# A two-layer encoder on one core: the probabilities of layer 1's attention turned by DMA instead of by TensorE, with the memory heads' halves, two output blocks and the memory loads moved beside it

## The chip, the core and the metric

The kernel runs on one core of a Trainium2 chip. Its time is the device time of one execution in microseconds (us). An execution taken with the profiler is described by its span, from the first to the last instruction, and by its own time, which is a little longer. Matrix products run on TensorE (PE in the profile, its weight loads PEld), elementwise work on VectorE (DVE) and ScalarE (ACT), a little on GpSimd (POOL). Weights are loaded by DMAs that SyncE (SP) issues; DMA transposes are issued from ACT's queue; small tables and the memory tokens come through POOL's queue. Every engine works through its own list of instructions strictly in order: an instruction that waits holds up all that stand behind it on its engine.

## What is computed

A trunk of two layers over 256 tokens of width 2048, all in f32. Layer 0 mixes tokens by a gated spatial product, layer 1 by grouped-query attention: 12 query heads of 128, 4 key and value heads, per-head RMS norm and rotary tables. Each layer also attends with 4 heads over 256 memory tokens; token heads and memory heads share one input and one output projection, and a SwiGLU feed-forward part follows.

```
h = rms_norm(x, g_mix[l])
z = h @ w_in_b                       # layer 1: queries, keys, values, memory queries
tok_out = softmax(q @ k.T * scale) @ v            # 12 heads, 256 x 256 each
kv = rms_norm(mem, g_mem[l]) @ w_mem_kv[l]
mem_out = softmax(q_mem @ k_mem.T * scale) @ v_mem    # 4 heads
x = x + concatenate([tok_out, mem_out]) @ w_out[l]
x = x + (silu(gate) * up) @ w_down[l]             # gate, up = rms_norm(x, g_ffn[l]) @ w_gate_up[l]
```

## The kernel before, in words

**Products.** f32 products are made from three fp32r products of halves (`matmul3`, L183 to L188): the high half of a times the high half of b (L186), low times high (L187), high times low (L188). The high half is a cast copy on ACT, the low half the difference on DVE. For activations that is `split` (L180 on ACT, L181 on DVE).

**Weights.** A weight matrix comes in blocks of 512 columns. A block is loaded as four *units* of four 128-row pieces, 1 MB each; I write in_b 23 for the last unit of the sixth block of `w_in_b`. `halves` makes a unit's two halves in two steps of 128x1024: `whi` on ACT (L270), then `wlo` on DVE (L271). Both have three tiles, so the halves of a unit can only be written when TensorE is through with the unit three before it. A unit is 24 matmuls of 128x512 into the two accumulators of its `Linear`. There are four accumulator banks in all, two for each block, so a block can start only when the block before the last has been read out of its banks. Four further banks (`m` in the names) serve transposes, scores and weighted sums.

**Layer 1's input stage.** In order: keys (in_b 0 to 3), values (4 to 7), three groups of four token heads called c0, c1 and c2 here (8 to 19), memory queries (20 to 23), then the memory keys (mem_kv 8 to 11), the memory values (mem_kv 12 to 15), and the four blocks of `w_out` (out 16 to 31). For each group of heads `queries` reads the accumulators (squares on ACT, L466; rotary on DVE, L474, L479 and L481, which free the banks), and `attend` then runs four kinds of steps: queries turned, scores with softmax (row maximum L557 on DVE, a product on POOL L558, exponentials L562 on ACT, reciprocal L566 and scaling L568 on DVE), probabilities turned, and weighted sums (`weigh`). Two heads make a step. The probabilities of a token head are turned by four TensorE transposes of 128x128 (L585) into an `m` bank, and split from there. Those of the memory heads go by DMA: `turned` (L194) copies the f32 words apart into two planes of 16 bits (128x1024, L199), issues a DMA transpose from ACT (L200), and three steps later copies back (L205).

**The order.** `later(n, step)` puts a step n *ticks* behind, two ticks to a weight unit; this sets the order in which the program states its work and its priorities. A scheduler then lays out each engine's list by its own costs, and that list is fixed: on the chip nothing is overtaken.

**Tiles.** A room of 36 tiles of 128x512 (`a` in the names) holds the stage's values. A second pool of 16 tiles (`h`) holds the normed input; after the last input unit (in_b 23) has been multiplied these are free.

Of the kernel before, what the change touches and what calls it, by code (L numbers as in the profile page):

```python
# [11 lines left out]
F32R = mybir.dt.float32r  # L12
# [5 lines left out]
P = 128  # L18
# [37 lines left out]
def encoder(ctx: ExitStack, tc: tile.TileContext, x, x_t, mem, mem_t, columns, w_in_a, g_v_a, spatial_t, w_in_b,  # L56
# [18 lines left out]
    def big(dt=F32, shape=None):  # L75
        return room["p"].tile(shape or [P, NB], dt, tag="a", name=nm("a"))
# [13 lines left out]
    def misc():  # L90
        if room["banks"] == 2:
            return banks2()[:, 0]
        return room["m"].tile([P, NB], F32, tag="m", name=nm("m"))

    def v4(a):
        return a.rearrange("p (c n) -> p c n", n=P)
# [80 lines left out]
    def split(src, shape, home=None):  # L177

        hi, lo = [(home or big)(F32R, shape) for _ in range(2)]
        nc.scalar.copy(hi, src)  # L180
        nc.vector.tensor_tensor(lo, src, hi.bitcast(F32), ALU.subtract)  # L181
        return hi, lo

    def matmul3(out, a, b, start, stop):

        nc.tensor.matmul(out, lhsT=a[0], rhs=b[0], start=start, stop=False)  # L186
        nc.tensor.matmul(out, lhsT=a[1], rhs=b[0], start=False, stop=False)  # L187
        nc.tensor.matmul(out, lhsT=a[0], rhs=b[1], start=False, stop=stop)  # L188
# [118 lines left out]
    def linear(parts, w, n0, units=kd, nk=KD):  # L307
        return Linear(parts, w, n0, nk).run(units)
# [202 lines left out]
            res.append(qn)  # L511
        return res

    def heads_T(qn, dma=False):

        hi = [big(F32R, [P, 2, S]) for _ in range(2)]
        lo = [big(F32R, [P, 2, S]) for _ in range(2)]

        def halves_of(t, whole):
            ts = slice(t * P, (t + 1) * P)  # L520
            for pr in range(2):
                src = whole[:, 2 * pr:2 * pr + 2, :]
                nc.scalar.copy(hi[pr][:, :, ts], src)
                nc.vector.tensor_tensor(lo[pr][:, :, ts], src, hi[pr][:, :, ts].bitcast(F32), ALU.subtract)

        for t in range(NT):
            if dma:
                turned(qn[t], 3, lambda whole, t=t: halves_of(t, whole), True, nc.vector.tensor_copy)
            else:
                tp = misc()  # L530
                transpose4(qn[t], tp)
                halves_of(t, v4(tp))
        return hi, lo

    def attend(qn, waits, keys, values, kv_of, kc0, parts, dma=None, home=None):


        qn, rows = qn
        by_head = rows.rearrange("p (t h) -> p h t", t=NT)
        st = {}  # L540

        def head(p, h):
            return p[0][h // 2][:, h % 2, :], p[1][h // 2][:, h % 2, :]

        def queries_T():
            st["qT"] = heads_T(qn, dma and home is None)

        def scores(pr):
            for h in (2 * pr, 2 * pr + 1):
                kp_ = head(keys(), kv_of(h))  # L550
                qp_ = head(st["qT"], h)
                sc = misc()
                for t in range(NT):
                    ts = slice(t * P, (t + 1) * P)
                    matmul3(sc[:, t * S:(t + 1) * S], (qp_[0][:, ts], qp_[1][:, ts]), kp_, True, True)
                nmx = small(2)
                nc.vector.tensor_reduce(nmx, sc.rearrange("p (t k) -> p t k", t=NT), AX.X, ALU.max, negate=True)  # L557
                nc.gpsimd.tensor_tensor(nmx, nmx, by_head[:, h], ALU.mult)  # L558
                pe = big()
                sm = small(2)  # L560
                for t in range(NT):
                    nc.scalar.activation(pe[:, t * S:(t + 1) * S], sc[:, t * S:(t + 1) * S], AF.Exp,  # L562
                                         bias=nmx[:, t:t + 1], scale=rows[:, 4 * t + h:4 * t + h + 1],
                                         accum_out=sm[:, t:t + 1])
                rcp = small(2)
                nc.vector.reciprocal(rcp, sm)  # L566
                for t in range(NT):
                    nc.vector.tensor_scalar(pe[:, t * S:(t + 1) * S], pe[:, t * S:(t + 1) * S], rcp[:, t:t + 1], None,  # L568
                                            ALU.mult)
                st["p", h] = pe  # L570

        def turn(pr):
            for h in (2 * pr, 2 * pr + 1):
                pn = st["p", h]
                if dma:
                    def halves_of(whole, h=h):
                        hi, lo = split(whole.rearrange("p (t k) n -> p k t n", t=NT), [P, 2, NT, P], home)
                        st["t", h] = [a.rearrange("p k t n -> p (k t n)") for a in (hi, lo)]

                    turned(pn, 3, halves_of, True, nc.vector.tensor_copy, home)  # L580
                    continue
                pt = misc()
                for t in range(NT):
                    for kc in range(2):
                        nc.tensor.transpose(pt[:, kc * S + t * P:kc * S + (t + 1) * P],  # L585
                                            pn[:, t * S + kc * P:t * S + (kc + 1) * P], ident)
                st["t", h] = split(pt, [P, NB])

        def weigh(pr):
            V = values()  # L590
            po = misc()
            for hh in range(2):
                h = 2 * pr + hh
                kv = kv_of(h)
                phi, plo = st["t", h]
                for kc in range(2):
                    vhi, vlo = V[kc]
                    vs, ks = slice(kv * P, (kv + 1) * P), slice(kc * S, (kc + 1) * S)
                    matmul3(po[:, hh * S:(hh + 1) * S], (vhi[:, vs], vlo[:, vs]), (phi[:, ks], plo[:, ks]),
                            kc == 0, kc == 1)  # L600
            hi, lo = split(po.rearrange("p (h s) -> p h s", h=2), [P, 2, S])
            for hh in range(2):
                for t in range(NT):
                    ts = slice(t * P, (t + 1) * P)
                    parts.put(kc0 + 2 * pr + hh, t, hi[:, hh, ts], lo[:, hh, ts])

        later(waits[0], queries_T)
        for wait, f in zip(waits[1:], (scores, turn, weigh)):
            for pr in range(2):
                later(wait + pr, lambda f=f, pr=pr: f(pr))  # L610

    def scaled(acc, r):

        res = []
        for t in range(NT):
            hi = big(F32R)
            lo = big(F32R)
            nc.scalar.activation(hi, acc[t], AF.Copy, scale=r[t])
            nc.vector.scalar_tensor_tensor(lo, acc[t], r[t], hi.bitcast(F32), ALU.mult, ALU.subtract)
            res.append((hi, lo))  # L620
        return res
# [2 lines left out]

    class Memory:
        def __init__(self, l):
            self.l, self.parts, self.r = l, Parts(), mem_r
            if l == 0:
                self.norm = Norm()

# [23 lines left out]
        def keys(self):  # L654
            acc = linear(self.parts, w_mem_kv[self.l], 0)
            kn = head_norm(acc, self.r, ghead[f"mk{self.l}"])

            def turn():
                self.kT = heads_T(kn, not self.l)
            later(4, turn)  # L660

        def values(self):
            self.V = scaled(linear(self.parts, w_mem_kv[self.l], NB), self.r)

        def attend(self, acc, r, parts, waits, dma, home=None):
            attend(queries(acc, r, ghead[f"mq{self.l}"]), waits, lambda: self.kT, lambda: self.V, lambda h: h, TOK // P,
                   parts, dma, home)

    def add_residual(acc, j, norm, g, parts, dma, copy=nc.scalar.copy):

# [20 lines left out]
    for l in range(DEPTH):  # L691
# [121 lines left out]
                    later(1 + t, lambda u=u, t=t, c=c: turn_u(u, t, c))  # L813
        else:
            w = w_in_b[0]
            own = {}
            load_tables(1)
            m.prep(20, 2)
            acc = linear(hT, w, TOK)
            kn = head_norm(acc, norm.r, ghead["k"], True)  # L820

# [11 lines left out]
            own["v"] = scaled(linear(hT, w, TOK + MEMW), norm.r)  # L833
            for c in range(3):
                acc = linear(hT, w, c * NB)
                attend(queries(acc, norm.r), (5, 6, 11, 14), lambda: own["k"], lambda: own["v"],
                       lambda h, c=c: (4 * c + h) // 3, 4 * c, cat)
            m.attend(linear(hT, w, TOK + 2 * MEMW), norm.r, cat, (4, 13, 16, 20), True, kept)
            m.keys()
            m.values()  # L840

        hF = Parts()
        norm = Norm()
        units = kd if l else [(12, KC4), (0, KC4), (4, KC4), (8, KC4)]
        for j in range(4):
            acc = linear(cat, w_out[l], j * NB, units)
            add_residual(acc, j, norm, gslice("ffn", l), hF, j < 3, nc.scalar.copy if l else nc.vector.tensor_copy)
        room.clear()
        scope.close()
# [130 lines left out]
```

## Time and profile before

| | us |
|---|---|
| median of 3 runs | 1986.66 (1985.84 to 1986.9) |
| the profiled execution's own time | 1988.33 |
| its span | 1986.5 |
| PE busy | 1975.7 (99%) |
| DVE busy | 1645.0 (83%) |
| ACT busy | 1217.9 (61%) |
| POOL busy | 95.7 (5%) |

The granted TensorE clock was 1.000 over the span. In the rows of a profile, `x16 | 10.9, 680` after an instruction's shape means 16 instructions, 10.9 us of busy time and 680 ns mean duration of one; behind the second bar stands how long the engine idled just before them and what ended that. Durations of consecutive instructions overlap a little on the chip; where I lay instructions end to end I use the distance of their starts. Layer 1's input stage stands at about 989 to 1320 us of the span.

### The profile page before, as it was taken

To read this page: it belongs to the slowest core of one execution; us is meant where nothing else is said; L and a number is where in the kernel's file an instruction comes from. 1 tells how busy PE (TensorE), PEld (TensorE's weight loads), DVE (VectorE), ACT (ScalarE), POOL (GpSimd) and SP (SyncE) were. 2 spreads that over 40 slices of the span, in tenths; PEclk is the share of its full clock that TensorE was granted. 3 is DMA by queue.
4 is the path that set the end of the run, shared out by engine and by line. 5 is a ranking of instruction groups with operands and counts; after the bars stand their busy time and mean duration, and the time that the engine had idled before them with its cause. 6 is when DMAs were issued, how large, how long until landed. Compare 5 with 4: busy or idle time off the path is not lost.

```text
span 1986.5 us, 24053 instructions
## 1 busy us (share of the span) xinstructions
PE 1975.7 (99%) x8897; PEld 1636.8 (82%) x8897; DVE 1645.0 (83%) x1755; ACT 1217.9 (61%) x1461; POOL 95.7 (5%) x148
## 2 busy tenths in 40 slices
PE   9999999999999999999999999999999999999998
PEld 7888888888888888888888888888888888888887
DVE  6658778998889989898676866699989889898987
ACT  8756455766546665466766665756665466654673
POOL 2300001000000000000020110010000000000000
PEclk9999999999999999999999999999999999999999
DMA  9867865576775777767866545657767667686674
GB/s 349 300 191 203 242 212 190 189 217 216 231 244 186 220 217 239 235 191 232 239 201 197 168 140 175 217 191 220 226 198 246 212 208 233 195 251 215 202 219 140
DMA packets 287719, 426.99 MB, mean 215 GB/s; under 512 B 93904, under 2 KB 94160, under 8 KB 287600
## 3 DMA queue, kind: packets, MB, share of 16 engines
q1 hardware_dynamic: 199808, 387.62, 58.8%
q10 hardware_dynamic: 82800, 20.91, 6.3%
q0 software_dynamic: 4992, 16.91, 3.8%
q8 instruction: 70, 1.15, 0.2%
q14 instruction: 49, 0.40, 0.1%
HBM read 394.45 MB, written 2.10 MB: 200 GB/s over the span
## 4 chain that ended last, share of the span: by engine, by line
PE 94%; DMA 2%; DVE 2%; ACT 1%; issue 1%; SPq 0%; DVEq 0%; ACTq 0%
PE acc L188 27%; PE acc L186 26%; PE acc L187 26%; PE m L188 5%; PE m L186 5%; PE m L187 5%; DMA a<-a 1%; DVE wlo L271 1%; DMA raw<-in_w_in_a 1%; PE m L192 0%; ACT whi L270 0%; PE m L722 0%; ACT junk L212 0%; PE m L585 0%; DVE T L379 0%
## 5 line engine op out<-in xcount | busy, mean ns | idle before, releaser
L271 DVE TENSOR_TENSOR wlo<-raw,whi 128x2048 fp32r<-128x2048 f32 (+2 forms) x466 | 841.4, 1821 | 202.9 <-ACT whi L270 198.8
L270 ACT CAST whi<-raw 128x2048 fp32r<-128x2048 f32 (+2 forms) x466 | 705.9, 1535 | 434.3 <-PE acc L187 294.5
L186 PE MATMUL acc<-whi,h 128*128 128x512 f32 x1440 | 561.6, 390 | 1.7 <-ACT whi L270 1.7
L187 PE MATMUL acc<-whi,h 128*128 128x512 f32 x1440 | 560.7, 389 | 0.0
L188 PE MATMUL acc<-wlo,h 128*128 128x512 f32 x1440 | 514.8, 390 | 0.1
L186 PE MATMUL acc<-whi,a 128*128 128x512 f32 x999 | 388.3, 390 | 1.0 <-DVE x L457 1.0
L187 PE MATMUL acc<-whi,a 128*128 128x512 f32 x999 | 388.6, 389 | 0.0
L188 PE MATMUL acc<-wlo,a 128*128 128x512 f32 x999 | 365.6, 390 | 0.4 <-DVE wlo L271 0.3
L188 PEld LDWEIGHTS acc<-wlo,h 128*128 128x128 f32 x1440 | 270.3, 188 | 57.9 <-DVE wlo L271 2.0
L186 PEld LDWEIGHTS acc<-whi,h 128*128 128x128 f32 x1440 | 270.4, 188 | 57.4 <-ACT whi L270 2.3
L187 PEld LDWEIGHTS acc<-whi,h 128*128 128x128 f32 x1440 | 270.4, 188 | 55.4
L188 PEld LDWEIGHTS acc<-wlo,a 128*128 128x128 f32 x999 | 187.5, 188 | 40.7 <-DVE wlo L271 2.1
L186 PEld LDWEIGHTS acc<-whi,a 128*128 128x128 f32 x999 | 187.6, 188 | 39.8 <-issue 1.4
L187 PEld LDWEIGHTS acc<-whi,a 128*128 128x128 f32 x999 | 187.6, 188 | 38.8
L270 ACT CAST whi<-T 128x1536 fp32r<-128x1536 f32 x93 | 137.8, 1481 | 119.2 <-PE acc L187 98.7
L271 DVE TENSOR_TENSOR wlo<-T,whi 128x1536 fp32r<-128x1536 f32 x93 | 162.9, 1751 | 4.7 <-PE acc L188 4.7
L379 DVE TENSOR_TENSOR T<-raw 128x1024 f32<-128x1024 f32 x93 | 113.4, 1219 | 19.8 <-DMA raw<-in_w_gate_up 19.7
L186 PE MATMUL m<-whi,a 128*128 128x512 f32 x284 | 110.7, 390 | 0.0
L187 PE MATMUL m<-whi,a 128*128 128x512 f32 x284 | 110.5, 389 | 0.0
L188 PE MATMUL m<-wlo,a 128*128 128x512 f32 x284 | 110.5, 389 | 0.0
L457 DVE TENSOR_TENSOR e<-acc,e 128x512 f32<-128x512 f32 x120 | 79.0, 684 | 1.5 <-PE acc L188 1.3
L205 ACT COPY sg<-a 128x1024 uint16<-128x1024 uint16 x44 | 51.5, 1171 | 30.7 <-DMA a<-a 30.5
(162 smaller groups left out, 1528.0 us busy)
## 6 DMA issues: line engine op xcount, KB each, us to landing
raw<-in_w_gate_up SPq DMA_DIRECT2D x352, 512.0 KB, 4.4
raw<-in_w_down SPq DMA_DIRECT2D x176, 512.0 KB, 5.1
raw<-in_w_out SPq DMA_DIRECT2D x32, 1024.0 KB, 5.3
raw<-in_w_in_a SPq DMA_DIRECT2D x24, 1024.0 KB, 8.0
raw<-in_w_in_b SPq DMA_DIRECT2D x24, 1024.0 KB, 5.1
raw<-in_w_mem_kv SPq DMA_DIRECT2D x16, 1024.0 KB, 5.2
x<-e POOLq DMA_DIRECT2D x16, 512.0 KB, 5.0
a<-in_mem_t POOLq DMA_DIRECT2D x16, 256.0 KB, 5.9
```

Of the source, the lines that this page charges most:

```text
L186: nc.tensor.matmul(out, lhsT=a[0], rhs=b[0], start=start, stop=False)
L187: nc.tensor.matmul(out, lhsT=a[1], rhs=b[0], start=False, stop=False)
L188: nc.tensor.matmul(out, lhsT=a[0], rhs=b[1], start=False, stop=stop)
L205: copy(halves, back.rearrange("p (h n) -> p n h", h=2))
L270: nc.scalar.copy(hi[:, cut], raw[:, cut])
L271: nc.vector.tensor_tensor(lo[:, cut], raw[:, cut], hi[:, cut].bitcast(F32), ALU.subtract)
L379: nc.vector.tensor_tensor(T[:, :2], raw[:, 1:4:2], w01, ALU.add)
L457: nc.vector.tensor_tensor(o[t][n], self.bank[name], o[t][n], op)
```

## The change

In layer 1:

- The probabilities of all 12 token heads are turned by DMA, with both copies on DVE, like those of the memory heads. The tuple `late` says which groups; it names all three. The 48 TensorE transposes of L585 go, and 12 DMA transposes and 24 DVE copies of 128x1024 come. For c2 the planes and halves lie in `h` tiles.
- The halves of the memory keys and of the memory values also lie in `h` tiles.
- The ticks after which a group weighs move from 14 to 16, 16 and 18 for the token groups and from 20 to 24 for the memory heads.
- The first two blocks of `w_out` run in turns, unit by unit, each in its own two banks.
- The eight loads of the memory tokens for layer 1 start 27 ticks into the stage instead of 20 (two ticks apart, as before). Each is scaled and split three ticks after its load (L242 on ACT, L243 on DVE).

In both layers the queries of all heads are split in one piece of 128x512 for each token tile instead of two of 128x256 (one ACT copy and one DVE difference instead of two and two).

```diff
-    def attend(qn, waits, keys, values, kv_of, kc0, parts, dma=None, home=None):
+    def attend(qn, waits, keys, values, kv_of, kc0, parts, dma, home, heads_dma):
...
+        def of_tokens(t, whole):
+            st["q", t] = split(whole, [P, 4, P], home if kc0 == TOK // P else None)
+
         def queries_T():
-            st["qT"] = heads_T(qn, dma and home is None)
+            for t in range(NT):
+                if heads_dma:
+                    turned(qn[t], 3, lambda whole, t=t: of_tokens(t, whole), True, nc.vector.tensor_copy)
+                else:
+                    tp = misc()
+                    transpose4(qn[t], tp)
+                    of_tokens(t, v4(tp))
...
-            self.l, self.parts, self.r = l, Parts(), mem_r
+            self.l, self.parts, self.r, self.home = l, Parts(), mem_r, kept if l else None
...
-                self.kT = heads_T(kn, not self.l)
+                self.kT = heads_T(kn, not self.l, self.home)
...
-            self.V = scaled(linear(self.parts, w_mem_kv[self.l], NB), self.r)
+            self.V = scaled(linear(self.parts, w_mem_kv[self.l], NB), self.r, self.home)
...
-            own = {}
+            own, late = {}, (0, 1, 2)
             load_tables(1)
-            m.prep(20, 2)
+            m.prep(27, 2)
...
-                attend(queries(acc, norm.r), (5, 6, 11, 14), lambda: own["k"], lambda: own["v"],
-                       lambda h, c=c: (4 * c + h) // 3, 4 * c, cat)
-            m.attend(linear(hT, w, TOK + 2 * MEMW), norm.r, cat, (4, 13, 16, 20), True, kept)
+                attend(queries(acc, norm.r), (5, 6, 11, (16, 16, 18)[c]), lambda: own["k"],
+                       lambda: own["v"], lambda h, c=c: (4 * c + h) // 3, 4 * c, cat, c in late,
+                       kept if c == 2 else None, False)
+            m.attend(linear(hT, w, TOK + 2 * MEMW), norm.r, cat, (4, 13, 16, 24), True)
...
+        both = [Linear(cat, w_out[l], j * NB) for j in range(1 + l)]
+        for unit in units:
+            for one in both:
+                one.run([unit])
         for j in range(4):
-            acc = linear(cat, w_out[l], j * NB, units)
+            acc = both[j].acc if j < len(both) else linear(cat, w_out[l], j * NB, units)
```

In the changed kernel the lines behind L512 have moved: the softmax is L564 (maximum), L565 (POOL), L569 (exponentials), L573 and L575.

How the lists move is shown at two places; a tile's number is its last part in a name.

**Place A, VectorE, where the memory keys begin.** Of the kernel before, from the reading of c2's accumulators (acc_8530, acc_8531) over the split of c1's first probabilities (a_8931) to the first low half of the memory keys (wlo_9189, mem_kv 8):

```order
L474 TENSOR_TENSOR a_8858<-acc_8530,a_7653 128x512
L479 TENSOR_TENSOR a_8860<-acc_8530,a_7653 128x8x32 x2
L474 TENSOR_TENSOR a_8865<-acc_8531,a_7653 128x512
L479 TENSOR_TENSOR a_8867<-acc_8531,a_7653 128x8x32 x2
L566 RECIPROCAL s_1462_8828<-s_1461_8825 128x2
L481 TENSOR_TENSOR a_8858<-a_8858,a_8860 128x512
L181 TENSOR_TENSOR a_8931<-m_8925,a_8930 128x512
L271 TENSOR_TENSOR wlo_9189<-raw_9186,whi_9188 128x1024
```

Of the changed kernel, from the low half of mem_kv 10 (wlo_9271), over the scaling of two heads of c1 (a_8730, a_8748) and the splits of c0's third and fourth probabilities (a_8758, a_8763) and of its first weighted sum (a_8792), to the reading of c2's first accumulator (here acc_8496):

```order
L271 TENSOR_TENSOR wlo_9271<-raw_9268,whi_9270 128x1024 x2
L573 RECIPROCAL s_1444_8734<-s_1443_8731 128x2
L564 TENSOR_REDUCE s_1446_8745<-m_8738 128x2
L575 TENSOR_SCALAR a_8730<-a_8730,s_1444_8734 128x256 x2
L573 RECIPROCAL s_1449_8752<-s_1448_8749 128x2
L575 TENSOR_SCALAR a_8748<-a_8748,s_1449_8752 128x256 x2
L181 TENSOR_TENSOR a_8758<-a_8425,a_8757 128x512
L181 TENSOR_TENSOR a_8763<-a_8443,a_8762 128x512
L181 TENSOR_TENSOR a_8792<-m_8778,a_8791 128x512
L243 SCALAR_TENSOR_TENSOR a_8796<-a_8614,cols,a_8795 128x256
L474 TENSOR_TENSOR a_8815<-acc_8496,a_7649 128x512
L479 TENSOR_TENSOR a_8817<-acc_8496,a_7649 128x8x32 x2
```

Before, c2's accumulators are read ahead of the low halves of every memory key unit; now they are read behind the third of them. TensorE's list at this place, in the changed kernel: the last three products of c0's second weighted sum (m_8852), and right behind them the first of the memory keys (mem_kv 8), into acc_9151, which has the bank of acc_8496. The twelve products of m_8852 and the twelve of c0's first sum (m_8778) stand in one piece behind the last product of in_b 23:

```order
L186 MATMUL m_8852<-a_8762,a_8070 128x256
L187 MATMUL m_8852<-a_8762,a_8071 128x256
L188 MATMUL m_8852<-a_8763,a_8070 128x256
L186 MATMUL acc_9151<-whi_9155,a_8387 128x512
L187 MATMUL acc_9151<-whi_9155,a_8388 128x512
```

**Place B, VectorE, where c1 is weighed.** Of the kernel before, from the splits of c1's second and third probabilities (out of `m` banks that TensorE filled) to the low half of mem_kv 10 (wlo_9311):

```order
L181 TENSOR_TENSOR a_8940<-m_8934,a_8939 128x512
L181 TENSOR_TENSOR a_8961<-m_8955,a_8960 128x512
L271 TENSOR_TENSOR wlo_9221<-raw_9218,whi_9220 128x1024 x2
L181 TENSOR_TENSOR a_8970<-m_8964,a_8969 128x512
L524 TENSOR_TENSOR a_8995<-m_8997,a_8993 128x2x128
L524 TENSOR_TENSOR a_8995<-m_9006,a_8993 128x2x128
L524 TENSOR_TENSOR a_8996<-m_8997,a_8994 128x2x128
L524 TENSOR_TENSOR a_8996<-m_9006,a_8994 128x2x128
L271 TENSOR_TENSOR wlo_9311<-raw_9308,whi_9310 128x1024 x2
```

Of the changed kernel, from the split of c1's first probabilities (a_9029) to that of the second (a_9034) and on into c2's softmax; wlo_9504 is mem_kv 14, the rows of L199 and L205 are c2's copies to planes and back:

```order
L181 TENSOR_TENSOR a_9029<-a_8656,a_9028 128x512
L199 COPY h_9226<-a_9019 128x1024
L271 TENSOR_TENSOR wlo_9504<-raw_9501,whi_9503 128x1024
L205 COPY a_9001<-h_9223 128x1024
L271 TENSOR_TENSOR wlo_9504<-raw_9501,whi_9503 128x1024
L181 TENSOR_TENSOR a_9034<-a_8674,a_9033 128x512
L205 COPY a_9019<-h_9227 128x1024
L573 RECIPROCAL s_1520_9071<-s_1519_9068 128x2
L564 TENSOR_REDUCE s_1522_9082<-m_9075 128x2
L575 TENSOR_SCALAR a_9067<-a_9067,s_1520_9071 128x256 x2
L199 COPY h_9242<-a_9067 128x1024
```

And from there to the splits of c1's third and fourth probabilities (a_9095, a_9100) and to the first operation on the memory queries (a_9146), which TensorE turns next:

```order
L205 COPY a_9067<-h_9243 128x1024
L573 RECIPROCAL s_1525_9089<-s_1524_9086 128x2
L181 TENSOR_TENSOR a_9095<-a_8730,a_9094 128x512
L575 TENSOR_SCALAR a_9085<-a_9085,s_1525_9089 128x256 x2
L181 TENSOR_TENSOR a_9100<-a_8748,a_9099 128x512
L199 COPY h_9246<-a_9085 128x1024
L181 TENSOR_TENSOR a_9129<-m_9115,a_9128 128x512
L494 TENSOR_TENSOR a_9146<-acc_8828,a_7652 128x512
```

Between the four splits of c1, whose sources were TensorE transposes before, there now stand a weight unit's two halves and three copies back, each of which waits for a DMA transpose of c2. TensorE's 24 products of c1's weighted sums (m_9115, m_9173) stand in one piece between the last product of mem_kv 11 and the four transposes of a_9146.

More of the change, by code (lines that the diff above doesn't have):

```diff
@@ L512, in head_norm, with heads_T @@
         return res
-    def heads_T(qn, dma=False):
-        hi = [big(F32R, [P, 2, S]) for _ in range(2)]
-        lo = [big(F32R, [P, 2, S]) for _ in range(2)]
+    def heads_T(qn, dma=False, home=None):
+        hi, lo = [[(home or big)(F32R, [P, 2, S]) for _ in range(2)] for _ in range(2)]
         def halves_of(t, whole):
@@ L550, in scores @@
                 kp_ = head(keys(), kv_of(h))
-                qp_ = head(st["qT"], h)
                 sc = misc()
                 for t in range(NT):
-                    ts = slice(t * P, (t + 1) * P)
-                    matmul3(sc[:, t * S:(t + 1) * S], (qp_[0][:, ts], qp_[1][:, ts]), kp_, True, True)
+                    qp_ = [a[:, h, :] for a in st["q", t]]
+                    matmul3(sc[:, t * S:(t + 1) * S], qp_, kp_, True, True)
                 nmx = small(2)
@@ L610, in attend, with scaled @@
                 later(wait + pr, lambda f=f, pr=pr: f(pr))
-    def scaled(acc, r):
+    def scaled(acc, r, home=None):
         res = []
         for t in range(NT):
-            hi = big(F32R)
-            lo = big(F32R)
+            hi, lo = [(home or big)(F32R, [P, NB]) for _ in range(2)]
             nc.scalar.activation(hi, acc[t], AF.Copy, scale=r[t])
@@ L658, in turn, with attend @@
             def turn():
-                self.kT = heads_T(kn, not self.l)
+                self.kT = heads_T(kn, not self.l, self.home)
             later(4, turn)
         def values(self):
-            self.V = scaled(linear(self.parts, w_mem_kv[self.l], NB), self.r)
-        def attend(self, acc, r, parts, waits, dma, home=None):
+            self.V = scaled(linear(self.parts, w_mem_kv[self.l], NB), self.r, self.home)
+        def attend(self, acc, r, parts, waits, dma):
             attend(queries(acc, r, ghead[f"mq{self.l}"]), waits, lambda: self.kT, lambda: self.V, lambda h: h, TOK // P,
-                   parts, dma, home)
+                   parts, dma, self.home, not self.l)
     def add_residual(acc, j, norm, g, parts, dma, copy=nc.scalar.copy):
```

## The prediction

> **What bounds the kernel now.** I read the page's busy shares first, then the engines' busy time by stretches of layer 1's input stage.
>
> ```profile
> PE 1975.7 (99%) x8897; PEld 1636.8 (82%) x8897; DVE 1645.0 (83%) x1755; ACT 1217.9 (61%) x1461; POOL 95.7 (5%) x148
> ...
> 1100.00:1140.00 40.00, 40.00 (x216) 34.16 (x215) 33.85 (x63) 25.49 (x60) 5.45 (x8) 1.00 0.51 164
> 1140.00:1180.00 40.00, 40.00 (x227) 34.71 (x226) 27.06 (x47) 28.15 (x75) 3.69 (x8) 1.00 0.42 135
> 1180.00:1220.00 40.00, 40.00 (x193) 33.68 (x192) 30.69 (x55) 22.33 (x39) 2.46 (x5) 1.00 0.65 193
> ```
>
> The columns are stretch, length, and busy time of PE, PEld, DVE, ACT and POOL. TensorE works without a gap where the change sits: 40.00 of every 40 us. So each matmul taken out shortens the run, and each time TensorE has to wait lengthens it by the whole wait. VectorE has 6 to 13 us of slack in 40, ACT 12 to 18: enough on average, so the question is whether what TensorE needs next is done in time, in lists that cannot be overtaken.
>
> **What is removed.** The first two lines are from the list of groups and the chain of waits; the others give the pace of 128x256 and 128x512 products.
>
> ```profile
> L585 PE MATMUL m<-ident,a 128*128 128x128 f32 x48 | 6.7, 272 | 0.0
> 1096.11 0.87 PE m L585 x8
> ...
> 1226.61 0.12 PE m L186
> ...
> 1226.97 0.23 PE acc L186
> ```
>
> Eight transposes hold TensorE for 0.87 us, 0.109 each (the 272 ns of the group overlap). 48 × 0.109 = **5.2 us** less, all on the path. Splitting queries in larger pieces, the other tiles for the memory halves and the output blocks in turns take nothing from TensorE; I cost them at nothing. They are covered by the slack of VectorE and ACT, and without it a 128x512 split would cost its 0.60 us.
>
> **What is added, and its prices.** 24 copies of 128x1024 on VectorE and 12 DMA transposes. The memory heads already do this, so their rows price it. First VectorE in order of time, then groups in 1060 to 1240 us.
>
> ```profile
> 1187.83 2.36 DVE L271 TENSOR_TENSOR wlo<-raw,whi 128x1024 fp32r<-128x1024 f32 x2 [1.48 <-ACT whi L270]
> 1190.11 1.61 DVE L524 TENSOR_TENSOR a<-m,a 128x256 fp32r<-128x256 f32 x4
> ...
> 1199.36 0.61 DVE L568 TENSOR_SCALAR a<-a,s 128x256 f32<-128x256 f32 x2
> 1200.01 0.69 DVE L199 COPY h<-a 128x1024 uint16<-128x1024 uint16 x1
> ...
> 1203.80 0.69 DVE L205 COPY a<-h 128x1024 uint16<-128x1024 uint16 x1 [0.74 <-DMA h<-h]
> 1204.41 0.16 DVE L566 RECIPROCAL s<-s 128x2 f32<-128x2 f32 x1
> 1204.49 0.67 DVE L557 TENSOR_REDUCE s<-m 128x2 f32<-128x512 f32 x1
> 1205.08 0.60 DVE L568 TENSOR_SCALAR a<-a,s 128x256 f32<-128x256 f32 x2
> ...
> L243 DVE SCALAR_TENSOR_TENSOR a<-a,cols,a 128x256 fp32r<-128x256 f32 x14 | 6.3, 477 | 0.0
> L558 POOL TENSOR_TENSOR s<-s,s 128x2 f32<-128x2 f32 x16 | 5.1, 320 | 92.1 <-DVE s L557 85.2 <-ACT junk L466 3.7 <-ACT whi L270 3.2
> L637 POOL DMA_DIRECT2D a<-in_mem_t x5 | 2.9, 572 | 0.3 <-issue 0.3
> ```
>
> From start to start: both halves of a `wlo` 2.28, a copy 0.61, reciprocal 0.08, row maximum 0.59, scaling of a head 0.65. A split's low half and L474 are as wide as the maximum's source; I set them at 0.60. L479 is as wide as L524, whose four rows take 1.61: 0.40. L243's 477 ns less the overlap of 0.08 give 0.40. A maximum takes about 0.4 to pass POOL (320 ns and the handing over). Now ACT, and the DMA transposes (median from issue to landing).
>
> ```profile
> 1174.62 1.99 ACT L270 CAST whi<-raw 128x1024 fp32r<-128x1024 f32 x2
> 1176.51 0.37 ACT L466 ACTIVATE junk<-acc,mem_r 128x128 f32<-128x128 f32 x1
> ...
> 1177.00 0.37 ACT L466 ACTIVATE junk<-acc,mem_r 128x128 f32<-128x128 f32 x1
> ...
> 1177.36 0.58 ACT L180 CAST a<-m 128x512 fp32r<-128x512 f32 x1
> 1177.82 0.38 ACT L466 ACTIVATE junk<-acc,mem_r 128x128 f32<-128x128 f32 x1
> ...
> 1197.46 0.56 ACT L562 ACTIVATE a<-m,s,s 128x256 f32<-128x256 f32 x1 [2.36 <-POOL s L558]
> ...
> 1198.02 0.56 ACT L562 ACTIVATE a<-m,s,s 128x256 f32<-128x256 f32 x1
> ...
> a<-a ACTq DMA_TRANSPOSE x74, 5.1
> h<-h ACTq DMA_TRANSPOSE x4, 3.1
> ```
>
> A pair of `whi` 1.89, a square 0.49 (0.36 ahead of another kind), a split's high half 0.46, a head's two exponentials 1.1. L242, of the same kind and half the width of a split, I set at 0.39. A transpose I take at 3.1 alone and 5.1 when others are in flight.
>
> The memory loads, moved seven ticks later on POOL's queue, hold POOL 0.57 us for each issue, between the softmax products; POOL idled 92 us ahead of those 16 products, so I cost the issues at nothing, and at up to 0.6 for a product that meets one. Their scalings (L242, L243) now fall among the heads' work, and those that stand ahead of a needed operation are counted below at their places.
>
> **Place A.** Let E be the end of in_b 23. The low and high halves of mem_kv 10 wait for E, since the three tiles are taken; behind them on ACT stand two heads' exponentials of c1, six squares, and the high halves that TensorE needs. ACT: 1.9 + 1.1 + four squares 1.8 + 1.1 + split 0.5 + square 0.4 + split 0.5 = E + 7.2 for c0's fourth high half; with a square, the split of the first weighted sum and an L242, E + 8.5. VectorE follows: that split until 7.8, the sum's until 8.7, L243 9.1, L474 9.7, two L479 **10.5**. Only then is c2's accumulator read and mem_kv 8 may start. TensorE reaches it after 24 products, 24 × 0.12 = E + 2.9. **Wait: 7.6 us.** Before, those reads stood ahead of mem_kv 8's low half and nothing waited.
>
> **Between.** VectorE then runs four copies to planes and four back with no `wlo` between. With landings at 3.1 for the first and 5.1 for the rest, its eight copies end at E + 26.3, wlo mem_kv 11 at 29.0, mem_kv 12 with a split on each side at 32.5, mem_kv 13 at 34.8. TensorE, from 10.5 with 96 products of 0.227, eight transposes and 24 scores, would be at E + 31.6 where it needs the second of those splits: 0.9 lost, and mem_kv 11 ends at F = E + 36.9.
>
> **Place B.** c2's first maximum stands behind mem_kv 13 and ends at 35.4, F − 1.5. With POOL 0.4 and exponentials 1.1 that head is ready to scale at F + 0.0; the second maximum ends 0.7, scaling 1.3, planes 1.9; the second head's exponentials end 2.2, its reciprocal, the third maximum and scaling 3.5, and the split a_9029, without which c1's sum cannot go on, 4.1. On ACT a split, a square and mem_kv 14's high halves stand ahead of the DMA transpose: issued 5.0, landed 8.1. VectorE waits for it between mem_kv 14's two low halves: copy 8.8, second half 9.9, split a_9034 10.5. The sum ends at F + 11.0 where it would at F + 1.4: **9.6 us**. Then: copy back 11.1, maximum 11.8, scaling 12.4, planes 13.0, transpose landed 16.2, copy 16.9, split 17.6, scaling 18.2, split a_9100 18.8. The second sum ends at 19.3 instead of 12.4: **6.9 us**. Planes, split and L494 follow, 0.6 each: the turn of the memory queries waits until 20.7, **1.4 us**. Behind that VectorE is ahead again, and from the output blocks' end on both lists are the same.
>
> **Sum.** 7.6 + 0.9 + 9.6 + 6.9 + 1.4 = 26.4 lost, 5.2 gained: +21.2. On the profiled execution's 1988.3 that is 2009.5; the median of the runs stands 1.7 below it, so **2008 us**. Bounds: if every transpose had landed when VectorE asks for it, B's waits fall from 9.6 and 6.9 to 7.3 and 3.9 (2.3 and 3.0 us of waiting for a landing go) and the 0.9 goes: 6.2 less, 2002. If also c1's exponentials and squares in A were done before E, A would fall to about 3.5: 1998. With 5.1 instead of 3.1 at each of B's three landings, 6 more, and with 2 at mem_kv 11: 2016.
>
> The Trainium skill, "VectorE: DVE Perf Modes", "The three transpose paths", gives 1309 ns for a DMA transpose of 128x128 and 390 for TensorE's, and its rules advise TensorE where the result may go to PSUM. This trace has 3.1 us for eight blocks at once. By the page's 1.3 B's two waited landings would come 1.8 us earlier each, an estimate of 2004 us. No run here shows a transpose of that size alone.
>
> **Rivals.** *The engines keep ahead.* For it: VectorE's 6 to 13 us of slack in 40, against 24 × 0.61 = 15 us of copies over some 160 us; before, no block waited. If the waits together stay under 1 us, the gain stands: 1981 to 1982. Against: average slack doesn't help a list in which a copy waiting on a DMA stands ahead of a split that TensorE needs. 0.15. *Half of it.* Only the first half of place B bites, 4 to 9 us in all, and eats the gain: 1983 to 1990. 0.1. *More waiting.* Transposes of c2 come within 3 us of one another and take 5 us and more, and mem_kv 11's low half comes too late: 2014 to 2022. 0.15. *A colder TensorE.* Between E and F + 20 TensorE would stand still four times for 4 to 6.5 us, longer than anywhere in the trace.
>
> ```profile
> 1.35 4.39 PE L748 MATMUL m<-ident 128*128 128x128 f32 x24 [1.35 <-POOL ident masks.py:199]
> ```
>
> At the start, out of rest, 24 matmuls of the transposes' size took 4.39 us, 0.18 each, not 0.109. If after each long stop some 3.5 us of work went at 0.6 of the pace, that adds 1.4 at A, and at B the same behind the last stop (what lies between is hidden in the waits): 2011. 0.1. The rule behind it is in the Trainium skill, "TensorE: Matmul & The Clock Gate", "Part 1": after an idle window of about 3.4 us the clock halves until it has been busy as long. This trace has no such stop inside, so it shows only the slow start. The forecast itself, 1998 to 2014, has 0.5.
>
> **Chances.** 0.2%, about 4 us, is what a measurement of this kernel tells from no change. Faster 0.15, same 0.1, slower 0.75. The range 1984 to 2021 leaves out the faster case and the far end; the forecast's own is 1998 to 2014.
>
> **What would show it.** In the changed profile TensorE should idle before the first product of mem_kv 8, released by L479 of VectorE, some 7 us; before products of c1's two sums, released by L181, some 10 and 7; and VectorE should wait for DMA h<-h ahead of L205 there. The stage should grow by some 21 us and nothing behind it change. No such idle time, with the stage 5 us shorter, makes me wrong; so does a wait on `wlo` in the output blocks instead.

## The result, and the profile after

The changed kernel takes 2013.35 us in the median of four runs (2010.94 to 2018.04), the kernel before 1986.78 beside it (1985.84 to 1987.98). The ratio is 1.0132, with a 95% interval of 1.0120 to 1.0145: slower by 26.6 us. The profiled execution has a span of 2016.3 us and was the longest of the four, so I first ask which part of it belongs to the change. The layer's two norms end in a short sum (L261) whose first row marks the beginning and the end of layer 1's input and output projection. Of the kernel before, then of the changed one, these rows of VectorE and, between them, TensorE's last product of the output blocks:

```profile
996.30 0.15 DVE L261 TENSOR_REDUCE s<-s 128x1 f32<-128x8 f32 x1
...
1291.21 0.39 PE L188 MATMUL acc<-wlo,a 128*128 128x512 f32 x1
...
1299.03 0.16 DVE L261 TENSOR_REDUCE s<-s 128x1 f32<-128x8 f32 x1
```

```profile
999.90 0.15 DVE L261 TENSOR_REDUCE s<-s 128x1 f32<-128x8 f32 x1
...
1317.86 0.39 PE L188 MATMUL acc<-wlo,a 128*128 128x512 f32 x1
...
1326.32 0.15 DVE L261 TENSOR_REDUCE s<-s 128x1 f32<-128x8 f32 x1
```

Between the two rows of L261 lie 302.7 us before and 326.4 now: **+23.7 in this stage**. Ahead of it the profiled execution had lost 3.6 and behind it about 2.5, mostly between 600 and 690 us and near 1880, with short waits for weights, where the change moves nothing. I call the distance of these two rows the stage from here on. Its last row is VectorE's, however, and it stands 5.5 to 9.3 us behind TensorE's last output product in the runs below, without a wait of TensorE in between. So I also give the way from the first row to that product, *to TensorE's end*: 294.9 us before and 318.0 now, +23.1. Where the two differ, this one says what TensorE lost. The busy times and the clock on the changed kernel's page:

```profile
PE 1983.9 (98%) x8849; PEld 1637.4 (81%) x8849; DVE 1657.9 (82%) x1769; ACT 1216.4 (60%) x1451; POOL 93.6 (5%) x148
...
PEclk9999999999999999999999889999999999999999
```

Two slices of the clock have fallen. The engines' time in the same stretches as before the change (length, busy time of PE, PEld, VectorE, ACT and POOL with their counts, granted clock, DMA share, GB/s):

```profile
1100.00:1140.00 40.00, 39.59 (x187) 32.17 (x185) 28.51 (x49) 21.48 (x51) 6.68 (x9) 1.00 0.76 205
1140.00:1180.00 40.00, 32.40 (x153) 26.81 (x152) 32.50 (x60) 23.12 (x59) 4.07 (x8) 0.87 0.54 161
1180.00:1220.00 40.00, 29.66 (x138) 24.66 (x138) 28.73 (x55) 20.52 (x49) 2.36 (x4) 0.79 0.38 107
```

TensorE, which had no gap in any of these stretches, now stands still for 18 us in two of them, and its granted clock falls to 0.87 and 0.79. VectorE is no busier than it was over the three stretches together (89.7 us against 91.6). The longest two groups of TensorE's waits in the stage, with their total, count and longest:

```profile
PE m L186 <- ACT a L180: 12.0, 6, 4.3
PE m L188 <- DVE a L181: 4.9, 4, 1.9
```

It waits for the halves of probabilities (L180, L181), and at the end of either stall, 0.6 and 0.4 us, for the reading of accumulators (L479, L494). TensorE in order of time at place A:

```profile
1139.80 0.39 PE L188 MATMUL acc<-wlo,h 128*128 128x512 f32 x1
1141.83 0.39 PE L186 MATMUL m<-a,a 128*128 128x256 f32 x1 [1.64 <-ACT a L180]
1142.05 0.28 PE L187 MATMUL m<-a,a 128*128 128x256 f32 x1
1143.70 0.58 PE L188 MATMUL m<-a,a 128*128 128x256 f32 x1 [1.36 <-DVE a L181]
...
1145.79 0.41 PE L188 MATMUL m<-a,a 128*128 128x256 f32 x1
1149.45 0.58 PE L186 MATMUL m<-a,a 128*128 128x256 f32 x1 [3.25 <-ACT a L180]
...
1153.54 0.50 PE L186 MATMUL acc<-whi,a 128*128 128x512 f32 x1 [0.64 <-DVE a L479]
```

in_b 23 ends at E = 1140.0, and the first product of the memory keys comes at 1153.5. In between stand 24 products of 0.12, 2.9 us: 10.6 lost. At place B:

```profile
1179.05 0.39 PE L188 MATMUL acc<-wlo,a 128*128 128x512 f32 x1
1181.41 0.39 PE L186 MATMUL m<-a,a 128*128 128x256 f32 x1 [1.97 <-ACT a L180]
...
1183.28 0.28 PE L188 MATMUL m<-a,a 128*128 128x256 f32 x1
1184.17 0.58 PE L186 MATMUL m<-a,a 128*128 128x256 f32 x1 [0.61 <-ACT a L180]
1184.55 0.41 PE L187 MATMUL m<-a,a 128*128 128x256 f32 x1
...
1187.71 0.41 PE L188 MATMUL m<-a,a 128*128 128x256 f32 x1
1192.45 0.58 PE L186 MATMUL m<-a,a 128*128 128x256 f32 x1 [4.33 <-ACT a L180]
...
1196.05 0.41 PE L188 MATMUL m<-a,a 128*128 128x256 f32 x1
1196.88 1.11 PE L192 MATMUL m<-ident,a 128*128 128x128 f32 x4 [0.42 <-DVE a L494]
1197.65 0.78 PE L186 MATMUL acc<-whi,a 128*128 128x512 f32 x1
1198.22 0.63 PE L187 MATMUL acc<-whi,a 128*128 128x512 f32 x1
1198.65 0.63 PE L188 MATMUL acc<-wlo,a 128*128 128x512 f32 x1
...
1200.74 0.39 PE L187 MATMUL acc<-whi,a 128*128 128x512 f32 x1
```

mem_kv 11 ends at F = 1179.3; mem_kv 12 begins at 1197.65. c1's 24 products and four transposes would take 3.3 us of these 18.4: 15.1 lost. And the products of mem_kv 12 come 0.43 apart instead of 0.23 until 1200.4: from 1197.65 to 1200.74 the first seven take 3.1 us instead of 1.6. That is 1.5 more.

### The profile page after: what moved, and what is told of

Its sections match the earlier page's. It is cut to its first block, busy times and chain, and to the rows that moved or that the text cites. A ratio compares the mean times of both kernels' runs of the same rounds, so it can differ in the third digit from the quotient of the medians.

```text
span 2016.3 us, 23953 instructions
## 1 busy us (share of the span) xinstructions
PE 1983.9 (98%) x8849; PEld 1637.4 (81%) x8849; DVE 1657.9 (82%) x1769; ACT 1216.4 (60%) x1451; POOL 93.6 (5%) x148
## 5 line engine op out<-in xcount | busy, mean ns | idle before, releaser
L205 ACT COPY sg<-a 128x1024 uint16<-128x1024 uint16 x44 | 51.5, 1171 | 33.9 <-DMA a<-a 33.9
```

What stands on the lines that cost most here:

```text
L205: copy(halves, back.rearrange("p (h n) -> p n h", h=2))
```

## The experiments

The runs of the kernel before spread by 11 us on the chips of the experiments (1987 to 1998), more than beside the changed kernel. I therefore give for each the ratio to the runs of before on the same chip, and from the profile the stage (302.7 before, 326.4 in the changed kernel) and the way to TensorE's end, as the difference from the kernel before (+23.1 in the changed kernel). A table at the end of this section has all runs, with what was lost at A and at B.

### Undoing each part

**All heads on TensorE again**, the rest of the change kept.

```diff
-            own, late = {}, (0, 1, 2)
+            own, late = {}, ()
...
-                attend(queries(acc, norm.r), (5, 6, 11, (16, 16, 18)[c]), ...
+                attend(queries(acc, norm.r), (5, 6, 11, 14), ...
```

> The changed kernel with the token heads' probabilities turned by TensorE again (late = (), their sums 14 ticks behind as before); the memory halves in h tiles, the output blocks in turns and the late memory loads stay. Theory (copies to planes and back and the later sums put the needed splits and the reading of c2's accumulators behind other work on VectorE and ACT): both stalls go, and with them the slow clock; the 48 transposes come back, 5.2 us. 1985 to 1990 us, TensorE busy in all of layer 1's input stage. Rival (the late memory loads, or the tiles and output blocks, hold TensorE up): most of the 26 us stays, above 2005.

Ratio 0.9992 (0.9979 to 1.0005); stage 300.4, to TensorE's end as before (0.0). TensorE's time in the stretches where the stalls were:

```profile
1140.00:1180.00 40.00, 40.00 (x218) 34.18 (x218) 30.47 (x50) 28.47 (x74) 3.05 (x8) 1.00 0.43 137
1180.00:1220.00 40.00, 40.00 (x205) 34.12 (x204) 31.80 (x56) 22.42 (x40) 2.31 (x5) 1.00 0.56 166
```

Both stalls and the slow clock are gone. The DMA-turned probabilities are a necessary part of the loss; the h tiles, the late memory loads and the blocks in turns alone cost nothing.

**The memory loads back at 20 ticks**, all else as in the change.

```diff
-            m.prep(27, 2)
+            m.prep(20, 2)
```

> The changed kernel with only the memory loads put back to 20 ticks. Theory: place B's list is the same on TensorE (24 products of c1's sums in one piece behind mem_kv 11, then the memory queries' transposes), so its 15 us and its slow clock stay; at place A c0's first sum moves into in_b 23 and only the second stands behind it, so A's 10.6 us shrink to 5 to 9. 2004 to 2012. Rival (the memory loads' scalings among the heads' work are the cause): 1981 to 1988.

Ratio 1.0074 (1.0048 to 1.0100); stage 311.6, to TensorE's end +11.3. TensorE by ten microseconds:

```profile
1140.00:1150.00 10.00, 8.90 (x47) 7.48 (x47) 10.00 (x19) 7.40 (x24) 2.27 (x2) 1.00 0.50 177
...
1170.00:1180.00 10.00, 4.30 (x17) 3.20 (x15) 9.45 (x20) 8.44 (x30) 1.72 (x4) 0.67 0.64 193
1180.00:1190.00 10.00, 5.43 (x19) 4.62 (x20) 7.73 (x19) 3.89 (x9) 0.70 (x2) 0.50 0.38 72
```

Place B is nearly as it was (14.5 lost), with the clock at half. Place A shrinks to 1.3 us, where I had expected 5 to 9. So the memory loads' new place is not a neutral edit: together with c0's DMA it makes nearly all of A.

**The output blocks one after the other**, the memory heads' sums at 20 ticks.

```diff
-        both = [Linear(cat, w_out[l], j * NB) for j in range(1 + l)]
+        both = [Linear(cat, w_out[l], j * NB) for j in range(1)]
-            m.attend(..., (4, 13, 16, 24), True)
+            m.attend(..., (4, 13, 16, 20), True)
```

> The changed kernel with the first two output blocks one after the other and the memory heads' sums 20 ticks behind, as before. Theory: TensorE's list at places A and B is the same to the row, so the time is the changed kernel's, 2010 to 2016. Rival (four accumulators held at once by two blocks in turns): 1990 or less.

Ratio 1.0165 (1.0146 to 1.0183); stage 331.1, to TensorE's end +27.0. Both stalls are there, as expected; the rival falls. TensorE's end is 3.9 later than in the changed kernel, above what I had expected, and 3.3 of it stand in one place among the output blocks, where TensorE waits for weight halves:

```profile
1296.09 0.39 PE L188 MATMUL acc<-wlo,a 128*128 128x512 f32 x1
1298.69 0.50 PE L186 MATMUL acc<-whi,a 128*128 128x512 f32 x1 [2.21 <-ACT whi L270]
```

The blocks in turns thus help here rather than hurt.

### Which heads

**c2 alone by DMA** (sums 14, 14 and 18 ticks behind).

```diff
-            own, late = {}, (0, 1, 2)
+            own, late = {}, (2,)
```

> The changed kernel with DMA for c2 alone (late = (2,), sums 14, 14 and 18 ticks behind). Theory: c0's and c1's splits come from TensorE's transposes, ahead of c2's copies, and c2's accumulators are read early, so neither stall; 16 transposes, 1.7 us, are saved. 1983 to 1988, no slow clock. Rival (every DMA-turned head costs VectorE time that TensorE ends up waiting for, a third of the 26 us): 1993 to 1997.

Ratio 0.9992 (0.9979 to 1.0006); stage 301.5, TensorE without a stall at A or B and its end 1.8 us earlier than before: 16 transposes at 0.11. c2's copies on VectorE cost TensorE nothing here.

**c0 alone** (sums 16, 14, 14) and **c1 alone** (14, 16, 14).

```diff
-            own, late = {}, (0, 1, 2)
+            own, late = {}, (0,)        # and, in the other kernel, (1,)
```

> The changed kernel with DMA for c0 alone (sums 16, 14 and 14 ticks behind; memory loads at 27). Theory: place A's list is the changed kernel's (both of c0's sums behind in_b 23, c2's accumulators read late), place B's is not, since c1's splits come from TensorE transposes. So A's loss of about 10 us with some slow clock, nothing like it at B, 1.7 us saved: 6 to 11 us above the kernel before. Rival (it is the number of copies on VectorE): a third of the 26 us, and spread over the stage.

> The changed kernel with DMA for c1 alone (sums 14, 16 and 14 ticks behind). Theory: nothing at A, as c0's sums stand at in_b 19 and 20 again; at B the 24 products stand in nearly one piece again and c1's splits behind mem_kv 14's low half and c2's softmax, but without c2's copies and their landings: 5 to 10 us lost there, 1.7 saved: 3 to 8 us above the kernel before. Rival (place B's loss is the landings of DMA transposes alone): at most 2 us above.

c0 alone: ratio 1.0053 (1.0036 to 1.0070), stage 313.5, to TensorE's end +10.6, as expected. 10.0 is lost at A and nothing at B; a wait for weight halves near 1223, 1.6 us, is about what the 16 transposes save:

```profile
1130.00:1140.00 10.00, 7.34 (x36) 5.82 (x35) 8.15 (x18) 8.44 (x20) 1.61 (x5) 1.00 0.54 176
1140.00:1150.00 10.00, 5.74 (x29) 5.50 (x27) 8.60 (x19) 7.69 (x28) 2.74 (x4) 0.51 0.52 178
```

c1 alone: ratio 1.0055 (1.0037 to 1.0073), stage 313.8, to TensorE's end +11.4. Nothing is lost at A and 11.1 at B, 7.2 of it waits and the rest half pace; here too 1.5 us of waiting for weight halves, near 1222, stand against the saved transposes. The first stop at B:

```profile
1164.53 0.39 PE L188 MATMUL acc<-wlo,a 128*128 128x512 f32 x1
1170.12 0.58 PE L186 MATMUL m<-a,a 128*128 128x256 f32 x1 [5.21 <-ACT a L180]
```

A belongs to c0 and B to c1. c1 alone lost more than the 3 to 8 that I had expected, although none of c2's copies and landings stood in its way there. The rival, that landings make B, is out.

**c0 and c1**, c2 on TensorE.

```diff
-            own, late = {}, (0, 1, 2)
+            own, late = {}, (0, 1)
```

> The changed kernel with c2 turned by TensorE again (late = (0, 1)). Theory: A as in the changed kernel, about 10 us; B without the copies and landings of c2 loses 5 to 10 us instead of 15, and the slow clock lasts less long: 10 to 18 us above the kernel before. Rival (the copies of c2 don't matter, c1's late softmax does): 22 to 27 us above.

Ratio 1.0098 (1.0080 to 1.0116), 19.8 us; stage 319.5, to TensorE's end +19.1. That is a little above the 10 to 18 that I had expected and below the rival's 22. c2's copies and landings, net of the transposes that they save, make 4 us by TensorE's end and 7 by the time, no more.

**c2 alone and the memory loads at 20 ticks.**

```diff
-            own, late = {}, (0, 1, 2)
+            own, late = {}, (2,)
-            m.prep(27, 2)
+            m.prep(20, 2)
```

> DMA for c2 alone and the memory loads back at 20 ticks; the h tiles and the output blocks in turns stay. Theory: no stall at A or B; 1.7 us from 16 transposes, and about a microsecond more, as the stage with all turned on TensorE stood 1.2 us below the kernel before. 2 to 4 us below the kernel before. Rival (copies cost TensorE anyway): at or above it.

Ratio 0.9989 (0.9976 to 1.0001); stage 300.5, TensorE's end 1.9 us earlier than before, the 16 transposes. In the time it can't be told from no change.

### What B waits for in the end

c1 alone showed that something other than c2's copies holds place B. In the changed kernel's lists the first reading of the memory queries' accumulators (L494) waits for a product in the middle of c1's second sum: its result (a_9146) goes into a tile of the room of 36, and the tile it gets is the one that holds the high half of c1's third probabilities (a_9094), whose last reader is the fifth of the twelve products of m_9173. The second reading gets the tile of c1's fourth probabilities (a_8748), free after their split. mem_kv 12 needs those accumulators, so TensorE has nothing else to do until c1 is weighed. The rows of that line in the changed kernel:

```profile
L494 DVE TENSOR_TENSOR a<-acc,a x4: 677/680/691, 103.8 to 1196.8; 128x512 f32<-128x512 f32 x4
```

The last reading starts at 1196.8, 57 us after in_b 23 had filled the accumulators. To test it I gave that result another tile and changed nothing else; the scheduler then laid out the lists anew.

```diff
-    def queries(acc, r, gain=None):
+    def queries(acc, r, gain=None, home=None):
...
-                qn = big()
+                qn = (home or big)(F32, [P, NB])
...
-            attend(queries(acc, r, ghead[f"mq{self.l}"]), waits, ...
+            attend(queries(acc, r, ghead[f"mq{self.l}"], self.home), waits, ...
```

> The changed kernel with one thing else: the two tiles into which the memory queries' accumulators are read lie in h tiles, not in the room of 36. Theory, now with its cause: at place B the reading of those accumulators (L494) waited for a tile that c1's second weighted sum set free, and mem_kv 12 waited for the accumulators; with a tile at hand that reading stands ahead of mem_kv 11 and TensorE has mem_kv 12 to 14 to work on while c1's splits come. B's 15 us and its slow clock go; A's loss stays in part (5 to 10 us): 1 to 7 us above the kernel before. Rival (c1's splits themselves, behind c2's copies and a weight unit, hold TensorE up): at least 20 us above.

Ratio 1.0047 (1.0031 to 1.0062), 9.3 us; stage 309.4, to TensorE's end +8.8, 14.2 us less than in the changed kernel. The same line in this kernel:

```profile
L494 DVE TENSOR_TENSOR h<-acc,a x2: 684/684/684, 1148.2 to 1151.5; 128x512 f32<-128x512 f32 x2
```

And its engines' time:

```profile
1140.00:1150.00 10.00, 3.97 (x20) 2.90 (x19) 9.33 (x20) 9.90 (x32) 1.10 (x3) 0.95 0.54 173
...
1160.00:1200.00 40.00, 40.00 (x207) 34.14 (x206) 32.45 (x53) 26.87 (x58) 3.83 (x6) 1.00 0.77 209
1200.00:1210.00 10.00, 8.25 (x44) 7.25 (x43) 8.81 (x17) 5.22 (x9) 0.00 (x0) 0.86 0.34 113
```

The accumulators are read 45 us earlier, and TensorE has no gap from 1160 to 1200, though all of c1 and c2 still come by DMA. That settles B: it is a tile that is missing, and c1's late splits cost nothing as soon as TensorE has other work. What is left is 6.7 at A with 1.6 of half pace behind it, 3.2 in c2's sums near 1205, again with half pace behind it, and about 2 for want of weight halves near 1226. The last two I had not expected, and so the time and TensorE's end lie 2 us outside the 1 to 7.

**The same with the memory loads at 20 ticks**, and **with c0 on TensorE besides** (sums 14, 16, 18).

```diff
-            m.prep(27, 2)
+            m.prep(20, 2)
-            own, late = {}, (0, 1, 2)   # in the second kernel only
+            own, late = {}, (1, 2)
```

> The same with the memory loads back at 20 ticks. Theory: A's loss is the 1.3 us that the run with the loads put back had there, B's is none; 48 transposes are saved: 2 to 5 us below the kernel before. Rival (B was c1's splits): 8 us above or more.

> The same with c0 turned by TensorE (late = (1, 2), c0's sums 14 ticks behind). Theory: c2's accumulators are read ahead of all the memory keys' low halves, as in the kernel before, so nothing waits at A either; 32 transposes, 3.5 us, are saved and about a microsecond besides: 3 to 5 us below the kernel before, TensorE busy throughout the stage. Rival: at or above it.

With all heads by DMA: ratio 0.9994 (0.9982 to 1.0006); stage 297.7, 5.1 below before. Of these 5.1, TensorE's end has 3.0, the 5.2 of the 48 transposes less 2.0 us of waiting (1.1 at A, 0.8 for weight halves); the rest is the place of the last row. Its rows:

```profile
997.38 0.15 DVE L261 TENSOR_REDUCE s<-s 128x1 f32<-128x8 f32 x1
...
1289.34 0.39 PE L188 MATMUL acc<-wlo,a 128*128 128x512 f32 x1
...
1295.04 0.15 DVE L261 TENSOR_REDUCE s<-s 128x1 f32<-128x8 f32 x1
```

The rival would have left it 8 us above. In the timed runs (1984.3 to 1997.6 against 1988.6 to 1998.5) a gain of this size doesn't stand clear. With c1 and c2 only: 1.0002 (0.9991 to 1.0013), stage 301.5, TensorE's end 0.7 earlier than before; the expected 3 to 5 us are not there, since 2 us of waits appear near 1214, 1.4 for weight halves and 0.5 for halves of the memory values. So the first of the two is the best version found by TensorE's end, about as fast as the kernel before by its time.

### All runs

Lost at A or B is the time from the end of the last product ahead of the place to the first behind it, less the products and transposes in between at full pace. Half pace behind the place is not in it.

| kernel | stage, us | to TensorE's end, us | against before | lost at A | lost at B |
|---|---|---|---|---|---|
| before | 302.7 | 294.9 | | 0 | 0 |
| the change | 326.4 | 318.0 | +23.1 | 10.6 | 15.1 |
| all heads on TensorE | 300.4 | 294.9 | 0.0 | 0 | 0 |
| loads at 20 ticks | 311.6 | 306.2 | +11.3 | 1.3 | 14.5 |
| output blocks one after the other | 331.1 | 321.9 | +27.0 | 10.7 | 14.4 |
| c2 alone | 301.5 | 293.1 | −1.8 | 0 | 0 |
| c0 alone | 313.5 | 305.5 | +10.6 | 10.0 | 0 |
| c1 alone | 313.8 | 306.3 | +11.4 | 0 | 11.1 |
| c0 and c1 | 319.5 | 314.0 | +19.1 | 9.8 | 10.0 |
| c2 alone, loads at 20 | 300.5 | 293.0 | −1.9 | 0 | 0 |
| another tile for L494 | 309.4 | 303.7 | +8.8 | 6.7 | 0 |
| the same, loads at 20 | 297.7 | 292.0 | −3.0 | 1.6 | 0 |
| the same, c0 on TensorE | 301.5 | 294.2 | −0.7 | 0 | 0 |

## Why the prediction was right

Direction, size and both places came out: 2013 against 2008, inside the forecast's own range. The terms one by one; the measured ones add up to 22.0 of the 23.1 by TensorE's end, and of the 26.6 by which the medians differ some 3.5 are not found in this stage:

| term | predicted us | measured us |
|---|---|---|
| transposes saved | −5.2 | −5.3 (three times the 1.77 of c2 alone) |
| place A | 7.6 | 10.6 |
| between A and B | 0.9 | 0.2 |
| place B, first sum | 9.6 | 7.2 |
| place B, second sum | 6.9 | 6.9 |
| place B, memory queries | 1.4 | 0.9 |
| half pace behind B | 0 (rival: 1.4 at each place) | 1.5 |

"Between" is the time from 1153.54 to 1179.28 less its 96 products, eight transposes and 24 scores, 25.6 us in all. The sums of B are the ends at 1187.93 and 1196.26 less 1.44 each; the memory queries' 0.9 is what is left of the 15.1. That the sum is so near is partly luck: A came out 3.0 larger than predicted and B's three terms 2.9 smaller.

**Place A was mis-sized in one step**: that ACT turns to mem_kv 10's high halves at E. It was still behind. ACT in order of time at E, and the first reading of the accumulators on VectorE:

```profile
1139.27 0.57 ACT L569 ACTIVATE a<-m,s,s 128x256 f32<-128x256 f32 x1
...
1141.16 0.61 ACT L180 CAST a<-a 128x512 fp32r<-128x512 f32 x1
...
1142.89 2.00 ACT L270 CAST whi<-raw 128x1024 fp32r<-128x1024 f32 x2
...
1152.13 0.68 DVE L474 TENSOR_TENSOR a<-acc,a 128x512 f32<-128x512 f32 x1
```

The exponentials of c1's second head, two scalings of the memory loads (L242) and the first splits of c0 come first, and the weights start 2.9 us after E. From there the chain ran as priced: 10.6 − 2.9 = 7.7, predicted 7.6. I had counted only what stands behind the weights and taken for granted that what stands ahead of them was done.

**Place B was too large by 2.4 in its first landing.** I had the DMA transpose issued behind mem_kv 14's high halves, as it stands in ACT's list. It went out before them:

```profile
1180.58 1.25 ACTq L200 DMA_TRANSPOSE h<-h  x1
...
1181.61 1.99 ACT L270 CAST whi<-raw 128x1024 fp32r<-128x1024 f32 x2
...
1184.43 0.69 DVE L205 COPY a<-h 128x1024 uint16<-128x1024 uint16 x1
...
1192.55 0.69 DVE L205 COPY a<-h 128x1024 uint16<-128x1024 uint16 x1 [2.25 <-DMA h<-h]
```

It had landed when VectorE came to the first copy back, which did not wait, and neither did the second. Only the third copy did, for 2.25 us, the 3.1 us of landing after its planes as priced.

**The cause behind place B was not in the prediction.** It followed the lists and their waits rightly, so the wait came out, and it priced L494 behind c1's splits as one more item of VectorE's list. That L494 stood there for want of a tile, and that TensorE was idle for want of the accumulators rather than of the splits, came only from the experiments. The lower bound, 11.2 us for B's two sums without landings, is near the 11.1 that c1 alone lost at B, though 3.9 of these are half pace, which the bound has not; and one tile takes it to none.

**The clock.** The rival of a colder TensorE was right in kind, and at B its price shows: 1.5 us behind the last stop. At A it is hidden; the products at half pace end before the accumulators are read. In B's second sum about 1.1 us are half pace (the ten products from 1193.96 on take 2.3 us instead of 1.2), hidden in the same way, since TensorE would have waited for L494 until 1196.88 all the same. What each other rival would have left: the engines did not keep ahead; landings were not slow (3.1 us at most for c2's), and B bit as a whole, not its first half.

What is open: why A needs both c0's DMA and the late memory loads. The four corners of that square are clear (lost at A, the other heads differing among the runs and L494's tile as in the change; c0 by DMA at 27 ticks: 9.8 to 10.7; c0 by DMA at 20: 1.3; c0 on TensorE at 27: none; neither, the kernel before: none). A room short of tiles would explain it as at B, and the lists fit: in the changed kernel the first reading of c2's accumulators (a_8815) gets the tile of a high half of c0's probabilities (a_8694), which c0's first sum reads last, and the second reading (a_8822) the tile of c0's third probabilities (a_8425), free after their split; c0's sums stand behind E there. In the kernel before the first reading also gets a tile that c0's sums free, but these are over by 1125, and the reading starts at 1128.3, 15.8 us ahead of the end of in_b 23. A kernel with another tile at A was not tried, so its cause stays argued.

## What to carry to other kernels

Before pricing work that is moved onto slower but idle engines, ask of each step in the lists which buffer its result goes into and who frees it: here a missing tile, not busy time, tied the reading of accumulators to the slowest chain, and one other tile gave back 14 us. An edit that prolongs the life of values can be paid where another step needs their tile, and a neutral-looking shift of loads into that stretch can double the price (+11.3 became +23.1). And a chain priced from a point in the list needs the time at which its engine reaches that point, not only the time at which its input is there.

## What the runs showed of the hardware

**TensorE's clock falls to half after stops, short ones together included.** In the changed kernel the granted clock was 1.00 until 1142.6, 0.50 from 1142.7 to 1152.8, 1.00 again until 1183.6 and 0.50 from 1183.7 to 1200.6, and products came 0.43 us apart instead of 0.23. With c1 alone it fell inside a single stop of 5.2 us: 1.00 until 1169.2, 0.50 from 1169.3. But in the changed kernel no such stop stands ahead of either fall. At A there were a stop of 1.6 us, two products and the beginning of the next stop. At B there were two stops of 2.0 and 0.9 us, each with products behind it, and the beginning of the next; the longest stop, 4.3 us until 1192.45, came when the products were already slow (1184.17 above). One stop of 2.2 us (until 1298.69, with the blocks one after the other) had no slow products behind it. Full pace returned 3.4 us after the last long stop at A (1149.45) and 3.8 us after the last one at B (1196.88). The rule of the Trainium skill, "TensorE: Matmul & The Clock Gate", "Part 1" (half clock after an idle window of about 3.4 us, full clock after about as long of work), agrees with the half pace, with the return and with c1 alone; the falls at A and B came with products inside the last 3.4 us.

**A DMA issue leaves ACT's queue ahead of copies that stand before it.** The transpose of c2's first head stands behind mem_kv 14's two high halves in ACT's list and was issued at 1180.58, while the first of these began at 1181.61. So "nothing is overtaken", as the description ahead of the prediction has it, holds for what ACT executes in these rows, and not for the moment at which a DMA on its queue goes out.
